# Keeping two weight blocks of a seven-product group in their buffers for a second use

## The chip, the cores and the metric

The kernel runs on one core of a Trainium2 chip. The metric is the device time of one execution in microseconds (us). The time before is the median of three runs, 2410.04 us (2409.96 to 2410.2).

## The reference

The reference is a decoder trunk of two layers in float32 with 512 positions and a model width of 1024. Each layer is a half-step SwiGLU feed-forward block, a parallel mixing of three attentions, and a second half-step feed-forward block. The change touches only the feed-forward blocks, of which there are four:

```python
def _swiglu(t, w_gate, w_up, w_down):
    return (jax.nn.silu(t @ w_gate) * (t @ w_up)) @ w_down

for l in range(DEPTH):                                   # DEPTH = 2
    f = _swiglu(_rmsnorm(h, ffn1_pre_g[l]), ffn1_w_gate[l], ffn1_w_up[l], ffn1_w_down[l])
    h = h + 0.5 * _rmsnorm(f, ffn1_post_g[l])
    ...                                                  # token mixing
    f = _swiglu(_rmsnorm(h, ffn2_pre_g[l]), ffn2_w_gate[l], ffn2_w_up[l], ffn2_w_down[l])
    h = h + 0.5 * _rmsnorm(f, ffn2_post_g[l])
```

The hidden width is 2816, that is 22 tiles of 128.

## The kernel before

**Split products.** Every matrix product is made of three matmuls of the type fp32r: each factor is split into a high part h and a low rest l, and `mm3` sums h·h, h·l and l·h (L205, L206, L207). For a weight, ScalarE casts the high part, `wh` (L179), and VectorE subtracts it from the raw weight to get `wl` (L180). Names in the trace carry the block of the network: a0 and a1 are the first feed-forward blocks of the two layers, c0 and c1 the second ones. The trace leaves buffer numbers out, so `ga`, `ua`, `da` stand for gate, up and down weights of a0 and a1, and `gc`, `uc`, `dc` for those of c0 and c1.

**Seven products in place of eight.** The first 16 hidden tiles are worked in two chunks of eight. In each chunk the gate product, the up product and the down product are made as a group of seven half-size products (a Strassen-like scheme of Winograd's form) in place of eight: `feature_products` and `feature_product` for gate (G) and up (U), `products` and `product` for down (D). Four feature groups and two down groups make up the chunks of one feed-forward block; the last six hidden tiles are worked plainly. The weight matrix of a group has four blocks, B00, B10, B01 and B11. The weight factor of each product is

| product n | factor | block fetched by the product | subtraction on VectorE (L315) |
|---|---|---|---|
| 0 | B00 | B00 | none |
| 1 | B10 | B10 | none |
| 2 | t = B01 - B00 | B01 (into t) and B00 | t |
| 3 | t = B11 - t | B11 | t |
| 4 | B11 | B11 | none |
| 5 | t - B00 (t as product 3 left it, result in the raw buffer) | B00 | raw |
| 6 | t = B10 - t | B10 | t |

Feature groups take the products in the order 0, 2, 1, 3, 4, 5, 6 (`ORDER`), down groups in the order 0 to 6. A feature product has 48 matmuls of 128x128 by 128x256, a down product 24 of 128x512.

**Units, buffers and the queue.** A `BlockUnit` is half a block: 512 KB, fetched by one DMA that SP issues (`block`, L293). Each product has two of them. `fetch` gets a buffer and issues the transfer; `load` makes the subtraction if there is one, splits the result (`split_from`), and calls `loaded`, which gives the buffer back and lets further transfers start:

```python
def loaded(self):
    self.raw = None
    Q.took(self.place, -1)
    Q.fetch_ahead()
```

The class `Queue` holds all products in the order of a written-out list, `PLAN`: G of chunk 0, U of chunk 0, G of chunk 1, U of chunk 1, then the seven products of D of chunk 0 and of chunk 1, two at a time between plain gate and up products of the hidden tiles 18 and 20. Before a product starts, `load_ahead` loads the weights of the next products, four units ahead. `fetch_ahead` issues transfers in the order of the units, and stops at the first unit whose ring has no room. There are two rings: `raw`, of two buffers, and `o`, of four buffers in the feature groups and two in the down groups. In a feature group the units take the places raw, o, o in turn; in a down group the first unit takes raw and the second o. The split weights `wh` and `wl` have four buffers each. The tile t is kept in two further buffers of the tag `o` over a group.

The order in which each engine works through its instructions is set when the kernel is built, by a scheduler that estimates times, and is fixed on the chip: each engine runs its own stream in order. It puts a few matmuls of a following product ahead of the last product of the one before.

**Taking the results away.** In feature groups, ScalarE copies finished sums (L762) or applies the activation, and VectorE adds or multiplies the others into `hr` (L764, L766, L771). In down groups, VectorE forms the sums of the first factors, `as` (L798 to L804), and adds products to `f` (L838, L842).

Of the kernel before, what the change touches and what calls it, by code (L numbers as in the profile page):

```python
# [22 lines left out]
def kernel(  # L23
# [39 lines left out]
    _, S, D = x.shape  # L63
# [3 lines left out]
    ND = D // P  # L67
# [35 lines left out]
    def stile(shape, tag, name, dt=F32R):  # L103
        return sb.tile(shape, dt, tag=tag, bufs=BUFS[tag], name=name)
# [4 lines left out]
    def pbank(tag, name):  # L109
        return ps.tile([P, S], F32, tag=tag, bufs=4, name=name)  # L110
# [92 lines left out]
    def mm3(pt, lh, ll, rh, rl, start, stop, free=False):  # L203

        nc.tensor.matmul(pt, lh, rh, start=start, stop=False, skip_group_check=free)  # L205
        nc.tensor.matmul(pt, lh, rl, start=False, stop=False, skip_group_check=free)  # L206
        nc.tensor.matmul(pt, ll, rh, start=False, stop=stop, skip_group_check=free)  # L207
# [24 lines left out]
    class Unit:  # L232


        def __init__(self, src, k0, nk, c0, ncol, name, scale=None):
            self.tags, self.place = ("wh", "wl"), "raw"
            self.src, self.k0, self.nk, self.c0, self.ncol, self.name, self.scale = src, k0, nk, c0, ncol, name, scale
            self.h = self.raw = None

        def waits(self):  # L240

            return self.raw is None and self.h is None

        def fetch(self):
            if not self.waits():
                return
            Q.took(self.place, 1)
            self.raw = stile([P, self.nk, self.ncol], self.place, "raw_" + self.name, F32)
            nc.sync.dma_start(self.raw[:], self.src[self.k0 * P:(self.k0 + self.nk) * P, self.c0:self.c0 + self.ncol]
                              .rearrange("(k p) c -> p k c", p=P))  # L250

        def load(self):
            if self.h is not None:
                return
            self.fetch()
            self.split_from(self.raw[:])
            self.loaded()
# [5 lines that stand above are left out]
# [11 lines left out]
    class BlockUnit(Unit):  # L274
# [9 lines left out]
        def __init__(self, n, src, rows, k0, nk, ncol, keep, name, place="raw"):  # L284
            super().__init__(src, k0, nk, 0, ncol, name)
            self.n, self.rows, self.keep, self.fetched, self.place = n, rows, keep, False, place

        def waits(self):
            return not self.fetched
# [6 lines left out]
        def fetch(self):  # L296
            if self.fetched:
                return
            self.fetched = True
            if self.n == 2:  # L300
                tc.keep_in_program_order(self.block(self.keep.get(self.k0), (0, 1)))
            Q.took(self.place, 1)
            self.raw = stile([P, self.nk, self.ncol], self.place, "raw_" + self.name, F32)
            self.block(self.raw[:], self.BLOCKS[self.n])

        def load(self):
            if self.h is not None:
# [282 lines left out]
    def ffn(l, src, wg, wu, wd, dst, name, spare, parked, plan, aside=None):  # L590
# [123 lines left out]
        def beside(gen, steps, every):  # L714

            for i, us_ in enumerate(gen):
                if i % every == every - 1:
                    next(steps, None)
                yield us_
# [55 lines left out]
        def feature_products(ci, up):  # L775

            w, nm = (wu if up else wg)[l, :, ci * FC * P:(ci + 1) * FC * P], f"{'gu'[up]}{name}_{ci}"
            keep = Keep(lambda k0: stile([P, 2, S], "o", f"t{nm}_{k0}", F32)[:])
            places = itertools.cycle(("raw", "o", "o"))
            for n in ORDER:  # L780
                uns = [BlockUnit(n, w, ND // 2, k, 2, S, keep, f"{nm}_{n}_{k}", next(places)) for k in range(0, ND // 2, 2)]
                run = lambda n=n, uns=uns: feature_product(ci, up, n, uns)
                early = ci == 0 and not up and n in ORDER[:4]
                yield uns, (lambda run=run: beside(run(), itertools.islice(st["some"], 1), 2)) if early else run
# [4 lines left out]
        def first_factor(ci, n):  # L789

            a = lambda i, j: hr[2 * ci + j][:, :, HALVES[i]]
            nm = f"{name}_{ci}_{n}"
            h, l = (stile([P, FC // 2, S // 2], "v", f"a{x}{nm}")[:] for x in "hl")
            if n == 2:
                st["s", ci] = stile([P, FC // 2, S // 2], "v", f"as{nm}", F32)[:]
            s = st.get(("s", ci))
            if n == 2:
                nc.vector.tensor_tensor(s, a(1, 0), a(1, 1), ALU.add)  # L798
            elif n == 3:
                nc.vector.tensor_tensor(s, s, a(0, 0), ALU.subtract)  # L800
            elif n == 4:
                nc.vector.tensor_tensor(s, a(0, 1), s, ALU.subtract)
            elif n == 5:
                nc.vector.tensor_tensor(s, a(0, 0), a(1, 0), ALU.subtract)  # L804
            src = (a(0, 0), a(0, 1), s, s, s, s, a(1, 1))[n]
            split(h, l, src)
            st["a", ci, n] = h, l

        def product(ci, n, uns):
            if n == 0 and ci == 0:  # L810
                RINGS["o"] = 2
                dst.begin()
            if n < 6:
                first_factor(ci, n + 1)
            if n in (0, 1, 2):
                st["b", SUM[n]] = [pbank("z", f"pd{name}_{ci}_{n}_{e}") for e in range(2)]
            pts = st["b", SUM[n]]
            if n == 1 and ci:
                for e in range(2):
                    nc.scalar.copy(pts[e][:], dst.fs[e][:, HF[0]])  # L820
            h, l = st["a", ci, n]
            opens, ends = n in (0, 2) or (n == 1 and not ci), n in (1, 4, 6)
            for un in uns:
                for k in range(un.nk):
                    kk = un.k0 + k
                    for e in range(2):
                        c = slice(e * P, (e + 1) * P)
                        mm3(pts[e][:], h[:, kk, c], l[:, kk, c], un.h[:, k], un.l[:, k], opens and kk == 0,
                            ends and kk == FC // 2 - 1, free=True)
                        yield 3 * S * PE_US  # L830
            if n == 0:
                return
            i, hf = TO[n]
            for e in range(2):
                f = dst.fs[2 * i + e][:, HF[hf]]
                if n == 1:
                    nc.scalar.copy(f, st["b", 0][e][:])
                    nc.vector.tensor_tensor(f, f, pts[e][:], ALU.add)  # L838
                elif ci == 0 and n in (2, 3, 6):
                    nc.scalar.copy(f, pts[e][:])  # L840
                else:
                    nc.vector.tensor_tensor(f, f, pts[e][:], ALU.add)  # L842

        def products(ci):

            keep = Keep(lambda k0: stile([P, 2, S], "o", f"bt{name}_{ci}_{k0}", F32)[:])
            w = wd[l, ci * FC * P:(ci + 1) * FC * P]
            for n in range(7):
                uns = [BlockUnit(n, w, FC // 2, k, 2, S, keep, f"d{name}_{ci}_{n}_{k}", ("raw", "o")[k // 2])
                       for k in range(0, FC // 2, 2)]  # L850
                yield uns, (lambda n=n, uns=uns: product(ci, n, uns))

        marks, made = {}, {}
# [16 lines left out]
        def queue(what):  # L870
            kind, n = what[0], what[1]
            if kind in "gu":
                if n not in made:
                    made[n] = plain(n)
                ms = (what[2],) if what[-1] in (0, 1) and len(what) == 3 else range(2)
                uns = made[n][kind == "u"]
                run = (lambda: gates(n, uns, ms)) if kind == "g" else (lambda: ups(n, uns, ms))
                Q.add(uns if ms[0] == 0 else [], run)
            elif kind == "a":
                Q.add([], lambda: iter(first_factor(n, 0) or ()))  # L880
            elif kind == "m":
                if name == "a0":
                    Q.add([], mem_stats)
            else:
                if what not in made:
                    made[what] = products(n) if kind == "d" else feature_products(n, kind == "U")
                for one in made[what]:
                    Q.add(*one)
                    break
# [746 lines left out]
```

## Time and profile before

| | before |
|---|---|
| median of 3 runs | 2410.04 us |
| the profiled execution | 2413.01 us, span 2411.3 us, granted clock 0.998 |
| TensorE busy | 2383.9 us (99%) |
| weight loads of TensorE busy | 2129.1 us (88%) |
| VectorE busy | 1865.6 us (77%) |
| ScalarE busy | 1357.8 us (56%) |
| DMA | 372.10 MB, 154 GB/s on average |
| transfers of the feed-forward weights | 512 KB each, 4.2 to 4.8 us from issue to landing (median) |

The profile is of one execution, which took longer than the median by 3 us. Busy time of TensorE is modelled, since matmuls overlap, so an idle time of TensorE is read from what it waited for. In the lists of instructions a time in brackets is the idle time of the engine just ahead of the instruction, and behind the arrow stands what ended it. The chain is followed from the last instruction back to what released each step.

### The profile page before, as it was taken

The numbers are of one execution on the slowest core, as the hardware profiler recorded it, in microseconds if no ns is written. First come the engines' busy times: TensorE is split into PE (matmuls) and PEld (weight loads), VectorE is DVE, ScalarE is ACT, GpSimd is POOL, SyncE is SP. The second block draws the span as 40 slices with busy tenths as digits, with TensorE's granted clock in tenths as the row PEclk, the third lists the DMA queues.
The fourth block names the chain that finished last, engine by engine and source line by source line (L and its number), as shares of the span: only waits on it lengthen the run. The fifth ranks groups of instructions, "written<-read, shape, count | busy, mean of one in ns | idle before, by whom it ended". The sixth has DMA issues, their size and how long they took to land.

```text
span 2411.3 us, 36506 instructions
## 1 busy us (share of the span) xinstructions
PE 2383.9 (99%) x14407; PEld 2129.1 (88%) x14407; DVE 1865.6 (77%) x2462; ACT 1357.8 (56%) x2137; POOL 81.5 (3%) x134
## 2 busy tenths in 40 slices
PE   9999999999999999999999999999999999999998
PEld 8998889888888899988899988889888888999887
DVE  8878877678776688788698788766778766887885
ACT  6555565567655555455554554656676655545554
POOL 1000000000110000000000000000001100000000
PEclk9999999999999999999999999999999999999999
DMA  6765454222223466655557655542222234676544
GB/s 236 229 198 185 157 193 140 79 71 71 82 68 114 149 217 201 209 174 176 186 183 227 202 184 174 189 118 71 71 88 74 63 127 150 200 230 198 176 156 157
DMA packets 249344, 372.10 MB, mean 154 GB/s; under 512 B 11450, under 2 KB 126162, under 8 KB 249172
## 3 DMA queue, kind: packets, MB, share of 16 engines
q1 hardware_dynamic: 249076, 369.74, 47.9%
q8 instruction: 113, 1.85, 0.3%
q14 instruction: 59, 0.48, 0.1%
q0 software_dynamic: 96, 0.03, 0.0%
HBM read 357.14 MB, written 12.58 MB: 153 GB/s over the span
## 4 chain that ended last, share of the span: by engine, by line
PE 84%; DVE 7%; DMA 4%; ACT 3%; issue 2%; SPq 0%; DVEq 0%; ACTq 0%
PE pg L205 3%; PE pg L206 3%; PE pg L207 3%; PE pda L206 3%; PE pda L207 3%; PE pda L205 3%; PE pdc L206 2%; PE pdc L207 2%; PE pdc L205 2%; PE pb L207 1%; PE pb L206 1%; PE pb L205 1%; DMA raw_wo<-in_w_out_dram 1%; PE pwc1g L205 1%; PE pwc0g L205 1%
## 5 line engine op out<-in xcount | busy, mean ns | idle before, releaser
L205 PE MATMUL pg<-us_a,wh_wg 128*128 128x512 f32 x384 | 151.7, 395 | 0.0
L206 PE MATMUL pg<-us_a,wh_wg 128*128 128x512 f32 x384 | 150.6, 392 | 0.0
L207 PE MATMUL pg<-us_a,wl_wg 128*128 128x512 f32 x384 | 150.5, 392 | 0.0
L206 PE MATMUL pda<-wl_da,aha 128*128 128x512 f32 x224 | 87.5, 391 | 0.7 <-DVE wl_da L180 0.7
L206 PE MATMUL pdc<-wl_dc,ahc 128*128 128x512 f32 x224 | 87.5, 391 | 0.5 <-DVE wl_dc L180 0.5
L207 PE MATMUL pdc<-wh_dc,alc 128*128 128x512 f32 x224 | 87.2, 389 | 0.0
L207 PE MATMUL pda<-wh_da,ala 128*128 128x512 f32 x224 | 87.2, 389 | 0.0
L180 DVE TENSOR_TENSOR wl_dc<-raw_dc,wh_dc 128x1024 fp32r<-128x1024 f32 x50 | 61.1, 1222 | 33.2 <-ACT wh_dc L179 32.6
L205 PE MATMUL pda<-wh_da,aha 128*128 128x512 f32 x224 | 86.5, 389 | 0.0
L205 PE MATMUL pdc<-wh_dc,ahc 128*128 128x512 f32 x224 | 86.5, 389 | 0.0
L207 PEld LDWEIGHTS pg<-us_a,wl_wg 128*128 128x128 f32 x384 | 72.7, 189 | 15.5
L205 PEld LDWEIGHTS pg<-us_a,wh_wg 128*128 128x128 f32 x384 | 73.0, 190 | 14.6
L206 PEld LDWEIGHTS pg<-us_a,wh_wg 128*128 128x128 f32 x384 | 72.9, 190 | 14.6
L179 ACT CAST wh_dc<-raw_dc 128x1024 fp32r<-128x1024 f32 x50 | 52.7, 1053 | 57.6 <-PE pdc L207 17.7
L183 DVE SCALAR_TENSOR_TENSOR wl_wg<-raw_wg,wh_wg 128x1024 fp32r<-128x1024 f32 x48 | 58.5, 1223 | 33.9 <-ACT wh_wg L182 33.6
L180 DVE TENSOR_TENSOR wl_da<-raw_da,wh_da 128x1024 fp32r<-128x1024 f32 x50 | 61.1, 1222 | 24.4 <-ACT wh_da L179 23.9
L179 ACT CAST wh_da<-raw_da 128x1024 fp32r<-128x1024 f32 x50 | 52.6, 1053 | 44.4 <-PE pda L207 17.6
L179 ACT CAST wh_uc<-raw_uc 128x1024 fp32r<-128x1024 f32 x44 | 46.2, 1049 | 51.0 <-PE pwc0u L206 12.6
L180 DVE TENSOR_TENSOR wl_uc<-raw_uc,wh_uc 128x1024 fp32r<-128x1024 f32 x44 | 53.8, 1222 | 25.6 <-ACT wh_uc L179 24.9
L179 ACT CAST wh_ua<-raw_ua 128x1024 fp32r<-128x1024 f32 x44 | 46.0, 1049 | 41.6 <-PE pwa1u L206 12.6
L180 DVE TENSOR_TENSOR wl_ua<-raw_ua,wh_ua 128x1024 fp32r<-128x1024 f32 x44 | 53.6, 1221 | 20.0 <-ACT wh_ua L179 19.3
L182 ACT ACTIVATE wh_wg<-raw_wg 128x1024 fp32r<-128x1024 f32 x48 | 50.8, 1061 | 26.6 <-PE pv L1044 13.5
(640 smaller groups left out, 8933.2 us busy)
## 6 DMA issues: line engine op xcount, KB each, us to landing
raw_da<-in_ffn_w_down_dram SPq DMA_DIRECT2D x74, 512.0 KB, 4.7
raw_dc<-in_ffn_w_down_dram SPq DMA_DIRECT2D x74, 512.0 KB, 4.8
raw_ga<-in_ffn_w_gate_dram SPq DMA_DIRECT2D x68, 512.0 KB, 4.5
raw_ua<-in_ffn_w_up_dram SPq DMA_DIRECT2D x68, 512.0 KB, 4.3
raw_gc<-in_ffn_w_gate_dram SPq DMA_DIRECT2D x68, 512.0 KB, 4.2
raw_uc<-in_ffn_w_up_dram SPq DMA_DIRECT2D x68, 512.0 KB, 4.3
raw_wg<-in_w_gate_dram SPq DMA_DIRECT2D x48, 512.0 KB, 3.5
raw_wo<-in_w_out_dram SPq DMA_DIRECT2D x24, 512.0 KB, 3.7
```

What stands on the lines that cost most here:

```text
L179: both = [nc.scalar.copy(h_ap, src)]
L180: make = lambda: nc.vector.tensor_tensor(l_ap, src, h_ap.bitcast(F32), ALU.subtract)
L182: both = [nc.scalar.activation(h_ap, src, AF.Copy, scale=scale)]
L183: make = lambda: nc.vector.scalar_tensor_tensor(l_ap, src, scale, h_ap.bitcast(F32), ALU.mult, ALU.subtract)
L205: nc.tensor.matmul(pt, lh, rh, start=start, stop=False, skip_group_check=free)
L206: nc.tensor.matmul(pt, lh, rl, start=False, stop=False, skip_group_check=free)
L207: nc.tensor.matmul(pt, ll, rh, start=False, stop=stop, skip_group_check=free)
```

## The change

In a feature group, product 2 uses the two raw buffers that product 0 filled with B00, and product 4 the two that product 3 filled with B11. In a down group, product 4 uses those of product 3; product 2 still fetches B00 again. A unit that gives its buffer on has an heir: when it is loaded it hands over the buffer in place of returning it, and the heir has no transfer of its own for it. The tile t is fetched as before. The turn of places raw, o, o now goes over the ten units that are left.

```diff
         def __init__(self, n, src, rows, k0, nk, ncol, keep, name, place="raw"):
             super().__init__(src, k0, nk, 0, ncol, name)
             self.n, self.rows, self.keep, self.fetched, self.place = n, rows, keep, False, place
+            self.heir = None
+
+        def inherits(self, un):
+            un.heir, self.place = self, None
...
             if self.n == 2:
                 tc.keep_in_program_order(self.block(self.keep.get(self.k0), (0, 1)))
+            if self.place is None:
+                return
             Q.took(self.place, 1)
             self.raw = stile([P, self.nk, self.ncol], self.place, "raw_" + self.name, F32)
             self.block(self.raw[:], self.BLOCKS[self.n])
+
+        def loaded(self):
+            if self.heir is None:
+                super().loaded()
+            else:
+                self.heir.raw, self.heir.place, self.raw = self.raw, self.place, None
...
-            places = itertools.cycle(("raw", "o", "o"))
+            places, had = itertools.cycle(("raw", "o", "o")), {}
             for n in ORDER:
-                uns = [BlockUnit(n, w, ND // 2, k, 2, S, keep, f"{nm}_{n}_{k}", next(places)) for k in range(0, ND // 2, 2)]
+                uns = [BlockUnit(n, w, ND // 2, k, 2, S, keep, f"{nm}_{n}_{k}", n in (2, 4) or next(places))
+                       for k in range(0, ND // 2, 2)]
+                if n in (2, 4):
+                    for un, of in zip(uns, had[n - 2 + (n == 4)]):
+                        un.inherits(of)
+                had[n] = uns
...
             for n in range(7):
                 uns = [BlockUnit(n, w, FC // 2, k, 2, S, keep, f"d{name}_{ci}_{n}_{k}", ("raw", "o")[k // 2])
                        for k in range(0, FC // 2, 2)]
+                if n == 4:
+                    for un, of in zip(uns, had):
+                        un.inherits(of)
+                had = uns
```

## The prediction

> **What bounds the kernel now.** I read the busy times first, then the chain that ended last, then the waits of TensorE, then windows of 40 us over the stages that hold the seven-product groups, and last the instructions of VectorE one by one around each wait. From the page, the busy times, the chain's shares and the DMA queue:
>
> ```profile
> PE 2383.9 (99%) x14407; PEld 2129.1 (88%) x14407; DVE 1865.6 (77%) x2462; ACT 1357.8 (56%) x2137; POOL 81.5 (3%) x134
> q1 hardware_dynamic: 249076, 369.74, 47.9%
> PE 84%; DVE 7%; DMA 4%; ACT 3%; issue 2%; SPq 0%; DVEq 0%; ACTq 0%
> ```
>
> TensorE is idle for 2411.3 - 2383.9 = 27.4 us in all, and the DMA engines are busy for less than half of the span. A change that takes transfers away and no matmul can gain only from these 27.4 us, and only from the part that stands in the touched stages. The waits of TensorE that stand there are these (the line with pdc holds one wait of 0.5 in c0's first down group and one of 0.8 in the rest of down, which has no groups):
>
> ```profile
> PE pdc L206 <- DVE wl_dc L180: 1.3, 2, 0.8
> PE pwa1g L207 <- DVE wl_ga L180: 1.2, 1, 1.2
> PE pda L206 <- DVE wl_da L180: 0.7, 1, 0.7
> PE pwc0g L207 <- DVE wl_gc L180: 0.7, 1, 0.7
> PE pwa0g L207 <- DVE wl_ga L180: 0.4, 1, 0.4
> PE pwc0u L205 <- DVE hrc L764: 0.2, 1, 0.2
> ```
>
> Each of them ends on VectorE, none on a DMA. The windows (busy time of PE, PEld, DVE, ACT, POOL, each with its count, then clock, DMA share, GB/s) give the same from the side of the idle time:
>
> ```profile
> 80.00:120.00 40.00, 39.43 (x326) 39.03 (x325) 31.92 (x38) 25.01 (x31) 0.00 (x0) 1.00 0.73 222
> 200.00:240.00 40.00, 39.31 (x184) 32.66 (x183) 34.59 (x33) 21.90 (x25) 0.00 (x0) 1.00 0.69 236
> 920.00:960.00 40.00, 40.00 (x335) 40.00 (x335) 30.72 (x30) 20.80 (x24) 0.00 (x0) 1.00 0.75 242
> 960.00:1000.00 40.00, 39.12 (x324) 38.72 (x323) 31.16 (x30) 18.73 (x22) 0.00 (x0) 1.00 0.66 200
> 2200.00:2240.00 40.00, 40.00 (x335) 39.97 (x334) 31.25 (x30) 22.29 (x27) 0.00 (x0) 1.00 0.56 184
> 1040.00:1080.00 40.00, 39.48 (x229) 34.65 (x228) 35.67 (x35) 18.46 (x21) 0.00 (x0) 1.00 0.56 198
> 1280.00:1320.00 40.00, 38.60 (x320) 38.20 (x319) 30.54 (x30) 17.78 (x21) 0.00 (x0) 1.00 0.67 204
> 2160.00:2200.00 40.00, 39.66 (x329) 39.26 (x328) 31.23 (x31) 18.44 (x22) 0.00 (x0) 1.00 0.68 203
> ```
>
> The idle time, 40 less PE's busy time, is 0.57 + 0.69 + 0.88 + 0.52 + 1.40 + 0.34 = 4.40 us. That is the most that the change can gain, and 0.18% of the run. The two windows without idle time hold 335 matmuls each, at a DMA share of 0.75 and of 0.56: the matmuls' own pace does not feel the transfers. So fewer bytes are worth nothing by themselves. What counts is when a weight's second factor (wl) is ready on VectorE.
>
> **What goes away.** A feature group loses four transfers of 512 KB (its third and its sixth product in order take over buffers), a down group two. Each of the four feed-forward blocks has four feature groups and two down groups, so 4 x (4 x 4 + 2 x 2) = 80 transfers, 42 MB of the 369.74 MB on the queue. No matmul, cast or subtraction goes or comes. By the rows above this costs and gains nothing directly. What it moves is the moment at which a buffer comes free, the moment of the next issue on SP, and the place that the scheduler then gives the subtractions (L315) in VectorE's in-order stream. I read these places off the built program's instruction order and price them on VectorE's timeline.
>
> **Where up meets gate (U of chunk 0, then G of chunk 1).** In c0 the timeline has, VectorE first, then one row of ScalarE, then two of the chain:
>
> ```profile
> 947.57 1.22 DVE L180 TENSOR_TENSOR wl_uc<-raw_uc,wh_uc 128x1024 fp32r<-128x1024 f32 x1
> ...
> 949.90 1.21 DVE L180 TENSOR_TENSOR wl_uc<-raw_uc,wh_uc 128x1024 fp32r<-128x1024 f32 x1
> 952.65 1.23 DVE L180 TENSOR_TENSOR wl_uc<-raw_uc,wh_uc 128x1024 fp32r<-128x1024 f32 x1 [1.53 <-ACT wh_uc L179]
> ...
> 958.68 1.23 DVE L315 TENSOR_TENSOR tgc<-tgc,raw_gc 128x1024 f32<-128x1024 f32 x1 [1.92 <-DMA raw_gc<-in_ffn_w_gate_dram]
> ...
> 961.56 1.22 DVE L315 TENSOR_TENSOR tgc<-tgc,raw_gc 128x1024 f32<-128x1024 f32 x1
> ...
> 965.68 1.22 DVE L180 TENSOR_TENSOR wl_gc<-raw_gc,wh_gc 128x1024 fp32r<-128x1024 f32 x1
> 966.82 1.28 DVE L764 TENSOR_TENSOR hrc<-hrc,pwc0u 128x512 f32<-128x512 f32 x2
> ```
> ```profile
> 963.09 1.05 ACT L179 CAST wh_gc<-raw_gc 128x1024 fp32r<-128x1024 f32 x1 [1.83 <-PE pwc0u L206]
> ```
> ```profile
> 956.79 4.25 DMA tgc<-in_ffn_w_gate_dram
> 967.55 0.39 PE pwc0u L205
> ```
>
> The cast of the next group's first weight is done at 963.09 + 1.05 = 964.14, yet its wl is made only from 965.68, because the two subtractions t = t - B00 at 958.68 and 961.56 (one waited 1.92 us for a DMA, and the queue behind it waited too) pushed the stream back. TensorE needs that wl for one matmul that the scheduler had put ahead of the last up product: the 0.7 us wait, and 0.2 us for the sum at 966.82 behind it.
>
> In the changed program both subtractions stand earlier: the first right behind the wl at 949.90, the second behind the one at 952.65. B00 needs no second transfer, and t's two transfers are released by the wl at 947.57 and at 949.90. With the 4.25 us of the tgc row, t lands at 947.57 + 1.22 + 4.25 = 953.0 and at 949.90 + 1.21 + 4.25 = 955.4. This adds a wait: VectorE, free at 951.1, stands until 953.0, and behind it is queued the wl now at 952.65, which moves to 954.2 and ends at 955.4. Who waits for that is the sixth product. Product seven begins at 967.55; less 0.9 us of waits, three matmuls ahead and 48 matmuls of 0.12 us (5.76), the sixth begins at about 960.5, so 5 us are spare. The wl after it ends at about 957.8, and its half begins at 963.4. By 958.4 VectorE has caught up. Two times 1.14 us then lie ahead of the congestion, the wl at 965.68 can start when its cast is done (964.2) and ends at 965.4, before TensorE comes to it (966.2). Besides, the matmul that needs it now stands behind the last product, 49 matmuls later. The 0.7 us go, in two independent ways. What is late next is the sum at 966.82, which can start no earlier than the matmuls that it reads are done; I take half of the 0.2 us as gone.
>
> The same reordering stands in all four blocks. Removed: 0.4 (a0) + 0.7 (c0) + 1.2 (a1) + 0 (c1, whose gate waits for no wl) = 2.3 us, and half of 4 x 0.2 = 0.4 us (the 0.2 is what the windows leave beside the wl waits of 0.4 and 1.2, and 0.34 in c1). Sum 2.7 us; bounds 1.5 and 3.2 (0.57 + 0.88 + 1.40 + 0.34).
>
> **Down, chunk 0.** Here VectorE is nearly full. Timeline, chain, and a window inside the burst of transfers:
>
> ```profile
> 1070.53 1.22 DVE L180 TENSOR_TENSOR wl_dc<-btc,wh_dc 128x1024 fp32r<-128x1024 f32 x1
> 1071.67 1.22 DVE L802 TENSOR_TENSOR asc<-hrc,asc 128x1024 f32<-128x1024 f32 x1
> 1072.80 1.22 DVE L315 TENSOR_TENSOR btc<-raw_dc,btc 128x1024 f32<-128x1024 f32 x1
> 1074.39 1.22 DVE L315 TENSOR_TENSOR raw_dc<-btc,raw_dc 128x1024 f32<-128x1024 f32 x1 [0.37 <-DMA raw_dc<-in_ffn_w_down_dram]
> 1075.54 1.22 DVE L180 TENSOR_TENSOR wl_dc<-btc,wh_dc 128x1024 fp32r<-128x1024 f32 x1
> ```
> ```profile
> 1064.62 0.37 SPq L293
> 1065.66 8.64 DMA raw_dc<-in_ffn_w_down_dram
> 1076.81 0.50 PE pdc L206
> ```
> ```profile
> 1066.00:1074.00 8.00, 8.00 (x37) 6.63 (x36) 7.80 (x8) 2.74 (x4) 0.00 (x0) 1.00 1.03 385
> ```
>
> Before, the second half of product 5 (issued 1065.66, landed 1074.30) is subtracted at 1074.39, ahead of wl of product 3 (1075.54), and TensorE waits 0.5 us for that. After, product 4 needs no transfer, product 5's first half takes its place on SP (issue about 1064.7), and its subtraction stands right behind the wl at 1070.53, ahead of the other subtraction (1072.80), of asc (1071.67) and of wl of product 3. VectorE is there at 1071.67. At 385 GB/s, 512 KB take 1.36 us; product 4's first half was two transfers ahead of the one landing at 1074.30, so it landed at 1074.30 - 2 x 1.36 = 1071.6. The added wait is about nothing, and three steps of 1.14 us later wl of product 3 starts at 1075.1, 0.4 us earlier than 1075.54. Its second half's wl comes about 0.8 us later than before, but two gate matmuls have been moved in front of it. I book 0.3 us gained over a0 and c0 together, of the 0.69 and 0.52 idle; bounds are +1.2 gained and the loss below. Down of chunk 1 has the same order and no wait of TensorE before; I take zero, with the same loss as a bound.
>
> **Sum.** 2.7 + 0.3 = 3.0 us off the profiled run of 2413.0 us, giving 2410.0. The profiled run is 3.0 us above the median of 2410.04, so the median goes to about 2407.0.
>
> **Rivals.** (1) Slower: product 5's first half lands late, with VectorE's stream standing behind its subtraction. If it takes the 8.64 us of the slowest row from 1065.0, it lands at 1073.6, 1.9 us after VectorE is there; less the 0.4 us of advance, wl of product 3 is 1.5 us later. With four blocks and two down groups each, the price is up to 8 x 1.5 = 12 us; with the 2.7 gained elsewhere that is 2410.0 + 9.3 = 2419.3 at worst, and 2416.3 with half of it in chunk 1's groups (4 x 1.5 + 4 x 0.75 - 2.7 = +6.3). It decides from a landing about 1 us late on average (8 x 1 - 2.7 = 5.3). For it: VectorE at 7.80 of 8 us, a0's and c0's existing waits. Against it: the place on the queue is product 4's, two ahead of the transfer that took 8.64 us. The Trainium skill (DMA: Bandwidth & Descriptors, Queues, rings and completion order) says that completion on one issuing queue need not be first in, first out; by that rule the earlier place promises nothing, and the landing could be as late as the burst's last. The rows shown here hold no two landings out of order, so this trace neither bears the rule out nor refutes it. (2) Nothing happens: the transfers were hidden, and the freed time on VectorE goes into other waits at the same places, 2410.0, or 2408.5 with the lower bound of 1.5. For it: the sum at 966.82 is right behind the wl. (3) Everything in the touched stages goes: 2410.0 - 4.4 = 2405.6. Against it: the sums must still be evacuated. (4) The buffers aren't taken over in all groups: then fewer than 80 transfers go; the built program has 80 fewer, so I give this no chance.
>
> **Chances.** Forecast (gain of 1.5 to 4.0) 0.53; nothing (within 1.5 either way) 0.20; everything 0.07; slower by (1) 0.20, of which 0.15 lie over the bound. A difference of 0.2%, 4.8 us, is about what a measurement of this kernel can tell from no change. Over that bound on the fast side I give 0.05, for idle time that the waits do not name; same 0.80. The range, 2405.0 to 2414.0, takes in (2), (3) and the milder half of (1).
>
> **What would show it.** Right: 80 transfers fewer; no wait of pwa0g, pwc0g, pwa1g for a wl; PE's idle time in 960 to 1000 below 0.3; a wait of tgc or tga for DMA of some 2 us on VectorE, earlier than before, that no PE wait follows. The down step is right if raw_d of product 5 is subtracted with less than 0.5 us of idle time before it. Wrong: a new PE wait on wl_d of product 3 or on wl_u of product 6 in order, a wait of over 1 us on raw_d ahead of L315, or another matmul count in windows without waits.

## The result, and the profile after

The change makes the kernel 0.2% faster: 2404.36 us (median of 20 runs, 2401.27 to 2407.39) against 2409.93 (20 runs, 2405.27 to 2412.84), a ratio of 0.9978 with a 95% interval of 0.9972 to 0.9984, so 3.9 to 6.7 us. A repetition gave 0.9980 (0.9971 to 0.9990). The direction was forecast; the size (3.0 us) and the low end of the range (2405.0) were not enough.

From the page of the full change, the counterparts of the busy times and the queue:

```profile
PE 2379.3 (99%) x14407; PEld 2127.5 (89%) x14407; DVE 1868.7 (78%) x2462; ACT 1356.5 (56%) x2137; POOL 81.5 (3%) x134
q1 hardware_dynamic: 227316, 327.79, 42.4%
```

The queue moved 369.74 - 327.79 = 41.95 MB less, which is 80 transfers of 512 KB. TensorE's busy time fell by 4.6 us although it has the same 14407 matmuls: a first sign that its busy time holds something that is not work. The windows of 40 us at the four places where up of chunk 0 meets gate of chunk 1:

```profile
80.00:120.00 40.00, 40.00 (x335) 39.97 (x335) 32.95 (x40) 24.51 (x31) 0.00 (x0) 1.00 0.54 164
960.00:1000.00 40.00, 40.00 (x335) 39.97 (x334) 31.73 (x30) 19.64 (x23) 0.00 (x0) 1.00 0.53 156
1280.00:1320.00 40.00, 40.00 (x335) 39.97 (x334) 33.03 (x32) 17.42 (x21) 0.00 (x0) 1.00 0.54 159
2160.00:2200.00 40.00, 40.00 (x335) 39.97 (x334) 30.08 (x28) 20.27 (x25) 0.00 (x0) 1.00 0.55 159
```

All four are without idle time and hold 335 matmuls, where before held 326, 324, 320 and 329. The start times of the same TensorE instructions in both profiles say the same: the full change gains 1.0, 1.3, 1.8 and 0.8 us at the four places, 4.9 us together. VectorE there, in c0 (this profile is 2.5 us ahead of that of before up to this place and 3.8 us ahead behind it, as the start times of the same ScalarE instructions in both show):

```profile
950.71 1.23 DVE L327 TENSOR_TENSOR tgc<-tgc,raw_gc 128x1024 f32<-128x1024 f32 x1 [2.20 <-DMA tgc<-in_ffn_w_gate_dram]
951.85 1.22 DVE L180 TENSOR_TENSOR wl_uc<-raw_uc,wh_uc 128x1024 fp32r<-128x1024 f32 x1
953.05 1.23 DVE L327 TENSOR_TENSOR tgc<-tgc,raw_gc 128x1024 f32<-128x1024 f32 x1
...
961.68 1.23 DVE L180 TENSOR_TENSOR wl_gc<-raw_gc,wh_gc 128x1024 fp32r<-128x1024 f32 x1 [0.76 <-ACT wh_gc L179]
962.88 1.41 DVE L776 TENSOR_TENSOR hrc<-hrc,pwc0u 128x512 f32<-128x512 f32 x2
```

Both subtractions of t stand early, VectorE waits 2.20 us for the first, nobody on TensorE waits for what is queued behind, and the wl of gate now waits for ScalarE's cast in place of VectorE's own queue. That is the mechanism as forecast. In down the waits stayed (waits of TensorE, full change):

```profile
PE pdc L206 <- DVE wl_dc L180: 0.7, 1, 0.7
PE pda L206 <- DVE wl_da L180: 0.5, 1, 0.5
```

### The profile page after: what moved, and what is told of

Its sections match the earlier page's. It is cut to its first block, busy times and chain, and to the rows that moved or that the text cites. A ratio compares the mean times of both kernels' runs of the same rounds, so it can differ in the third digit from the quotient of the medians.

```text
span 2402.7 us, 36336 instructions
## 1 busy us (share of the span) xinstructions
PE 2379.3 (99%) x14407; PEld 2127.5 (89%) x14407; DVE 1868.7 (78%) x2462; ACT 1356.5 (56%) x2137; POOL 81.5 (3%) x134
## 3 DMA queue, kind: packets, MB, share of 16 engines
q1 hardware_dynamic: 227316, 327.79, 42.4%
## 4 chain that ended last, share of the span: by engine, by line
PE 87%; DVE 6%; ACT 3%; DMA 3%; issue 1%; SPq 0%; DVEq 0%; ACTq 0%
PE pg L205 3%; PE pg L206 3%; PE pg L207 3%; PE pda L206 3%; PE pda L207 3%; PE pda L205 3%; PE pdc L206 2%; PE pdc L207 2%; PE pdc L205 2%; PE pb L207 1%; PE pb L206 1%; PE pb L205 1%; PE pwc0u L205 1%; PE pwc1u L205 1%; PE pwa1u L205 1%
```

## The experiments

**First: which groups bring it?** Four kernels take buffers over in some groups only. The edits go into the two lines with `n in (2, 4)` and the line `if n == 4` of down.

feats_only leaves out the three lines of down; down_only has `n in (2, 4) and False`; g1_only leaves out down and has

```diff
-                if n in (2, 4):
+                if n in (2, 4) and (ci == 1 and not up):
```

and all_but_g1 has `not (ci == 1 and not up)` and keeps down.

feats_only: 

> Only the feature groups take buffers over (64 transfers fewer), the down groups are as before. Theory A (the time comes from one place in each feed-forward block, where the last up product of chunk 0 meets the first gate product of chunk 1): -4.9 us, since the four windows around that place hold 326, 324, 320 and 329 matmuls before in place of 335, that is 41 matmuls of 0.119 us. Theory B (the time comes from the bytes, 5.6 us for 80 transfers, 0.07 us each): -4.5 us. Theory C (the down groups give or take): -5.6 less their share, so a gain clearly under 4 or over 6.

down_only: 

> Only the down groups take buffers over (16 transfers fewer). Theory A: 0 within 0.5 us, with TensorE still waiting 0.5 to 0.7 us for wl of product 3 in chunk 0 of a0 and c0. Theory B: -1.1 us. Theory C: whatever feats_only lacks to -5.6.

g1_only: 

> Only the gate group of chunk 1 takes buffers over, in each of the four blocks: 16 transfers fewer. Theory A: the whole -4.9 us, with 335 matmuls in each 40 us around the four places. Theory B: 16 x 0.07 = -1.1 us.

all_but_g1: 

> All groups take buffers over, but for the gate group of chunk 1: 64 transfers fewer. Theory A: 0 within 0.5 us, the waits for wl of gate (0.4, 0.7, 1.2) are still there. Theory B: 64 x 0.07 = -4.5 us.

Measured against before: feats_only 0.9985 (0.9976 to 0.9994), -3.6 us, with an interval (1.4 to 5.8 us faster) too wide to tell the three theories apart. down_only 1.0005 (0.9996 to 1.0014), not told from zero. g1_only 1.0016 (1.0007 to 1.0025), 3.9 us slower, with 16 transfers fewer. all_but_g1 1.0028 (1.0016 to 1.0040), 6.8 us slower, with 64 transfers fewer. Theory B (bytes) falls with the last two. Theory A in its simple form falls too: the gate group of chunk 1 alone puts VectorE's two subtractions early, but makes it worse. The timeline of VectorE in g1_only says why; it waits for both tiles t, and in the full change for the first alone:

```profile
952.16 1.23 DVE L327 TENSOR_TENSOR tgc<-tgc,raw_gc 128x1024 f32<-128x1024 f32 x1 [2.63 <-DMA tgc<-in_ffn_w_gate_dram]
...
958.35 1.23 DVE L327 TENSOR_TENSOR tgc<-tgc,raw_gc 128x1024 f32<-128x1024 f32 x1 [2.70 <-DMA tgc<-in_ffn_w_gate_dram]
```

and in its waits of TensorE the sums queued behind come late:

```profile
PE pwa0u L205 <- DVE hra L776: 2.0, 1, 2.0
PE pwc0u L205 <- DVE hrc L776: 1.7, 1, 1.7
PE pwc1u L205 <- DVE hrc L776: 1.5, 1, 1.5
PE pwa1u L205 <- DVE hra L776: 1.4, 1, 1.4
```

SP's issues of the second tile t in g1_only, and of both tiles in the full change (whose profile is 0.6 us ahead of that of g1_only there), say when the transfers could start:

```profile
954.55 0.37 SPq L297 DMA_DIRECT2D tgc<-in_ffn_w_gate_dram  x1
```
```profile
945.65 3.25 SPq L297 DMA_DIRECT2D tgc<-in_ffn_w_gate_dram  x2
```

With up of chunk 0 as before, buffers come free later, t lands after VectorE reaches its subtraction, and the added wait that was harmless in the full change stops TensorE. all_but_g1 keeps the waits for wl of gate (0.9, 0.5, 1.0) and adds four others of 1.0 to 1.5 us at the meetings of other groups.

**Second: which take-over, and which groups together?** Down stays as before in all three; `before_again` is the kernel before for a second profile.

```diff
-                if n in (2, 4):
+                if n in (2, 4) and up != ci:      # u0g1_only; n2_only has n == 2, n4_only has n == 4
```

u0g1_only: 

> The up group of chunk 0 and the gate group of chunk 1 take buffers over, 32 transfers fewer; where they meet, VectorE's order is that of the full change. Theory A2 (at that place both groups are needed: the gate group to put its two subtractions early, the up group so that SP can issue their transfers early; a stop of TensorE costs its wait plus about 0.27 us): -4.9 us there, with 335 matmuls in each of the four windows, and new waits only elsewhere. Theory B (0.07 us for each transfer): -2.2 us everywhere. Theory D (the gate group alone decides, and the loss of g1_only came from somewhere else): a loss as in g1_only, +4.6 us.

n2_only: 

> In all feature groups product 2 takes over, product 4 fetches again; down as before; 32 transfers fewer. VectorE's order where up of chunk 0 meets gate of chunk 1 is that of the full change. Theory A2: there the transfers of t are not issued earlier than the up group's own transfers allow, so waits of over 1 us for hr (L776) come back as in g1_only, about +2 us in all four against before at most, and no -4.9. Theory B: -2.2 us.

n4_only: 

> In all feature groups product 4 takes over, product 2 fetches again; down as before; 32 transfers fewer. TensorE's order is that of before, matmul for matmul. Theory A2: the matmul that needs wl of gate still stands ahead of the last up product and one subtraction still stands in the stretch ahead of that wl, so waits of 0.4 to 1.2 us for wl of gate stay, and the time is that of before within 1.5 us. Theory B: -2.2 us.

before_again: 

> The kernel before, unchanged, for a second profile of it: which steps of the comparison of two profiles stand in stages that no transfer was taken from. Theory A2: the steps at the start, near 590, near 1180 and near 1790 us (up to 1.8 us each) come and go from one execution to the next, and the four places where up meets gate stay within 0.5 us of the first profile.

u0g1_only is 1.0021 (1.0010 to 1.0031), n2_only 1.0035 (1.0021 to 1.0048), n4_only 1.0033 (1.0020 to 1.0045). In sum all three lose, but not in the same place. u0g1_only and n2_only have 332 or more matmuls in each of the four windows: where up meets gate they are as good as the full change. So theory A2 was right that the up group's take-over is needed beside the gate group's, and wrong on n2_only: product 2's take-over is enough for it. Their loss is a new stop at the end of gate of chunk 0 in all four blocks (waits of TensorE in n2_only; u0g1_only has the same four rows):

```profile
PE pwa0g L205 <- ACT sa L774: 1.9, 1, 1.9
PE pwc1g L205 <- ACT sc L774: 1.5, 1, 1.5
PE pwc0g L205 <- ACT sc L774: 1.5, 1, 1.5
PE pwa1g L205 <- ACT sa L774: 1.5, 1, 1.5
```

There the built kernel has matmuls of the sixth and fifth gate product interleaved in another order than before. n4_only keeps TensorE's order and has the waits for wl of gate, larger than before (1.6, 1.5, 0.9, 0.8). Theory A2 had put its time within 1.5 us of before; it is 8.0 us slower, and that forecast missed.

The second profile of before missed what I expected of it in part. The step at the start (1.4 us between the two profiles of before) and one near 1188 us (1.1 us, with a wait of 0.8 us for wl in the first) do come and go. Those near 590 and 1790 us stand in both; what they are is said at the end. But the loss that I meant to explain comes and goes as well: its four windows hold 331, 334, 316 and 335 matmuls.

```profile
960.00:1000.00 40.00, 39.97 (x334) 39.77 (x333) 30.56 (x30) 18.55 (x22) 0.00 (x0) 1.00 0.65 198
1280.00:1320.00 40.00, 38.15 (x316) 37.75 (x315) 31.70 (x32) 15.78 (x18) 0.00 (x0) 1.00 0.64 196
```

In the first profile of before 41 of 4 x 335 matmuls are missing there, in the second 24, in down_only (which leaves these groups alone) 33; at 40 / 335 = 0.119 us each that is 4.9, 2.9 and 3.9 us.

**Third: does the corrected theory predict a kernel?** n2_only was given product 4's take-over in gate of chunk 0 only, where its new stop was; g0u0g1 leaves out up of chunk 1 and down.

```diff
-                if n in (2, 4):
+                if n == 2 or n == 4 and (ci, up) == (0, False):   # n2_g0n4
...
-                if n in (2, 4):
+                if n in (2, 4) and (ci, up) != (1, True):         # g0u0g1
```

n2_g0n4: 

> n2_only with one thing more: in the gate group of chunk 0 product 4 takes over as well. TensorE's order is then that of before but for the one matmul moved in each block. 40 transfers fewer than before. Theory A3: the four waits of 1.5 to 1.9 us for ScalarE's sa and sc at the end of gate of chunk 0, which n2_only has, are gone (4 x 1.9 = 7.6 us with the 0.27 us of each stop), and the 335 matmuls where up meets gate stay: 3 to 5 us faster than before. Theory E (the half-changes are slower for their transfers, not for that order): as n2_only, about 8 us slower than before.

g0u0g1: 

> Both take-overs in the feature groups of gate 0, up 0 and gate 1, not in up 1, down as before; 48 transfers fewer. TensorE's order is before's but for the one matmul moved in each block. Theory A3: 3 to 5 us faster than before, unless the meeting of gate 1 and up 1 stops TensorE as it did in all_but_g1 (2 to 4 us for each block that does).

after_again: 

> The full change again, with a second profile. Theory A3 (product 2's take-over in the up group of chunk 0 and the gate group of chunk 1 takes the stop away where they meet; product 4's take-over keeps the other junctions as they were): faster than before by 3.5 to 6.5 us; 335 matmuls in each of the four windows again.

All three kernels came out as theory A3 said: n2_g0n4 0.9982 (0.9973 to 0.9991), g0u0g1 0.9981 (0.9971 to 0.9991), and the full change 0.9980 (0.9971 to 0.9990). Eight transfers fewer than in n2_only, two in each block, turn 8.4 us of loss into 4.3 us of gain, which bytes can't do. Theory A3 doesn't cover everything: n4_only and all_but_g1 stop at other junctions although product 4 takes over in most of their groups or in all, and why they do stays open. The windows of n2_g0n4:

```profile
80.00:120.00 40.00, 39.75 (x331) 39.55 (x330) 32.22 (x39) 24.33 (x30) 0.00 (x0) 1.00 0.63 187
960.00:1000.00 40.00, 40.00 (x335) 39.98 (x335) 31.66 (x30) 19.76 (x23) 0.00 (x0) 1.00 0.60 182
1280.00:1320.00 40.00, 40.00 (x335) 39.97 (x334) 33.16 (x33) 17.43 (x21) 0.00 (x0) 1.00 0.61 184
2160.00:2200.00 40.00, 40.00 (x335) 39.97 (x334) 29.98 (x28) 20.30 (x25) 0.00 (x0) 1.00 0.62 185
```

The whole of it in one table. Missing matmuls are those of 4 x 335 in the four windows; us are worked out from the ratio. The last column goes over the feature groups alone.

| kernel | transfers fewer | against before, us | missing matmuls (us at 0.119) | waits in other places of the feature groups that before has not |
|---|---|---|---|---|
| before, first and second profile | 0 | | 41, 24 (4.9, 2.9) | |
| full change | 80 | -5.3, again -4.8 | 0, 1 (0.1) | none |
| feats_only | 64 | -3.6 | 1 (0.1) | none |
| n2_g0n4 | 40 | -4.3 | 4 (0.5) | none |
| g0u0g1 | 48 | -4.6 | 6 (0.7) | none over 0.4 |
| down_only | 16 | +1.2 (-1.0 to +3.4) | 33 (3.9) | none |
| g1_only | 16 | +3.9 | 62 (7.4) | none over 0.5 |
| u0g1_only | 32 | +5.1 | 3 (0.4) | 1.9, 1.5, 1.5, 1.5, 0.7 for sa, sc |
| n2_only | 32 | +8.4 | 0 | the first four of these; 1.1 for wh |
| n4_only | 32 | +8.0 | 73 (8.7) | 1.1, 0.8, 0.7 for sa, sc |
| all_but_g1 | 64 | +6.8 | 40 (4.8) | 1.5 for wh; 1.4, 1.4, 1.0 for sa, sc |

Of the 73 missing matmuls of n4_only some 14 are none of its waits: in its window of c0, which holds 305, the granted clock is 0.50 for 3.4 us (968.2 to 971.6). Half of 3.4 us at 0.119 us each makes the 14, an estimate.

**Fourth: the stop in down.** pool3 is the full change with one sum moved:

```diff
             elif n == 3:
-                nc.vector.tensor_tensor(s, s, a(0, 0), ALU.subtract)
+                (nc.vector if ci else nc.gpsimd).tensor_tensor(s, s, a(0, 0), ALU.subtract)
```

pool3: 

> The full change with one more: in down of chunk 0 the sum as for product 3 is made by GpSimd in place of VectorE, four instructions of 1.1 us off VectorE's stream. If TensorE's waits there (0.5 and 0.7 us in a0 and c0, with 0.17 us of restart each) come from VectorE's full stream, they go, 1 to 1.5 us off the full change; if GpSimd takes over 4 us for the sum, the low part of the factor comes late and TensorE waits for that, 2 us or more slower.

It took back the gain: 1.0003 (0.9994 to 1.0011) against before, 5 to 6 us slower than the full change. GpSimd's group of instructions and TensorE's waits:

```profile
L817 POOL TENSOR_TENSOR asc<-asc,hrc 128x1024 f32<-128x1024 f32 x2 | 6.8, 3382 | 651.9 <-ACT wh_gc L179 651.9
```
```profile
PE pdc L206 <- DVE wl_dc L180: 3.3, 3, 1.7
PE pda L206 <- DVE wl_da L180: 2.6, 2, 1.3
```

The sum takes 3.4 us there in place of 1.2, still under the 4 us that I had set as the limit, and the waits grew from 1.2 to 5.9 us. The low part of the factor now stands later in VectorE's stream (at 1069.75 in c0) and the wl that TensorE waits for comes behind it, at 1074.30. So taking 1.1 us off VectorE here is not worth 1.1 us; that its stream is too full in this stage was not refuted by this.

## Why the prediction was wrong in size, point by point

**The step that failed is "The idle time, 40 less PE's busy time, is ... That is the most that the change can gain".** It took the idle time of TensorE in a window as the loss, and so the term of the four places where up meets gate, booked at 2.7 us with a bound of 3.2, came out at 4.9. The list of TensorE's instructions in before, across the stop in c0, shows the error:

```profile
965.89 0.28 PE L205 MATMUL pwc0g<-us_b,wh_gc 128*128 128x256 f32 x1
966.01 0.28 PE L206 MATMUL pwc0g<-us_b,wh_gc 128*128 128x256 f32 x1
966.96 0.38 PE L207 MATMUL pwc0g<-us_b,wl_gc 128*128 128x256 f32 x1 [0.66 <-DVE wl_gc L180]
967.55 0.39 PE L205 MATMUL pwc0u<-us_b,wh_uc 128*128 128x256 f32 x1 [0.22 <-DVE hrc L764]
967.78 0.28 PE L206 MATMUL pwc0u<-us_b,wh_uc 128*128 128x256 f32 x1
967.90 0.28 PE L207 MATMUL pwc0u<-us_b,wl_uc 128*128 128x256 f32 x1
```

Matmuls start 0.12 us apart and each row is 0.28 us long or more, since they overlap. Idle time is counted from the end of a row, so a stop shows less than it costs. From 966.01 to 967.78 there are three steps that take 1.77 us in place of 0.36: a loss of 1.41 us, of which the brackets show 0.88. The full change has no such gap: its window holds 335 matmuls. In c1 the prediction put the wait for wl at zero, since no row there shows one, and booked 0.1 us in all:

```profile
2163.96 0.28 PE L206 MATMUL pwc1g<-us_b,wh_gc 128*128 128x256 f32 x1
2164.36 0.39 PE L207 MATMUL pwc1g<-us_b,wl_gc 128*128 128x256 f32 x1
2164.96 0.39 PE L205 MATMUL pwc1u<-us_b,wh_uc 128*128 128x256 f32 x1 [0.21 <-DVE hrc L764]
2165.19 0.28 PE L206 MATMUL pwc1u<-us_b,wh_uc 128*128 128x256 f32 x1
```

The matmul with wl stands 0.40 us behind the one before it, without a bracket, and the three steps take 1.23 us in place of 0.36: a loss of 0.87 us, of which the brackets show 0.21. Counting matmuls gives the loss without this error, as long as the granted clock stays at 1.00, and the counts stood in the rows of the prediction: 335 - 326, 324, 320 and 329 are 9, 11, 15 and 6, 41 in all, 4.9 us in place of the 3.2 that I took as the upper bound of this term. So did the busy time of the weight loads: 40 less 39.03, 38.72, 38.20 and 39.26 is 4.8 us. The Trainium skill (Perfetto Trace Analysis, Identifying the Most-Contended Engine) says that matmul busy time is no good measure of how close a kernel is to the roofline, because pipelined instructions look smaller in the trace, and sends its reader to the busy share of weight loads, and to the share of the peak FLOP rate that a kernel reaches. Here the trace agrees, to 0.1 us in 4.9. Idle time falls short of the loss in the two other profiles with these groups as before too: 2.1 us of idle time against 2.9 us by count in the second profile of before, and 2.3 against 3.9 in down_only. That the loss went past the bound of 3.2 us, and not only past the booked 2.7, is a matter of the execution: in one of the three it did not.

**Where up meets gate: right in mechanism, too small in size.** Booked 2.7 us (0.5, 0.8, 1.3 and 0.1 in a0, c0, a1 and c1); the loss that is gone was 4.9 (1.0, 1.3, 1.8 and 0.8) in the profile I used, and 2.9 to 4.9 over three profiles that have these groups as before. The sum at 966.82, of whose 0.2 us I took half, cost nothing any more in any of the four blocks. That the gain has "two independent ways" was not shown: no kernel here moved the matmul and left the subtractions, or the reverse. The added wait of VectorE was forecast to end at 953.0 and, with the 2.5 us added back, ended at 953.2; the 5 us spare covered it.

**Down: booked at 0.3 us, found at nothing that can be told.** Product 5's first half landed in time (its subtraction follows the wl without idle time), so rival (1) fell. But wl of product 3 started at 1071.66, which is 0.07 us earlier than before, not 0.4:

```profile
1059.87 1.23 DVE L327 TENSOR_TENSOR btc<-btc,raw_dc 128x1024 f32<-128x1024 f32 x1 [0.74 <-DMA raw_dc<-in_ffn_w_down_dram]
...
1068.25 1.22 DVE L327 TENSOR_TENSOR raw_dc<-btc,raw_dc 128x1024 f32<-128x1024 f32 x1
1069.39 1.22 DVE L327 TENSOR_TENSOR btc<-raw_dc,btc 128x1024 f32<-128x1024 f32 x1
1070.53 1.22 DVE L819 TENSOR_TENSOR asc<-hrc,asc 128x1024 f32<-128x1024 f32 x1
1071.66 1.22 DVE L180 TENSOR_TENSOR wl_dc<-btc,wh_dc 128x1024 fp32r<-128x1024 f32 x1
```

The step was right that one wait of 0.37 us for a DMA goes; the first subtraction of the group waited 0.32 us longer (0.74 in place of 0.42) and gave it back. Second profile of before: 0.3 us of wait in c0 and none listed in a0, so this term also varies by itself more than I booked.

**Rivals and cover.** Rival (3), everything in the touched stages, came true where gate and up meet, and its price of 4.4 us was short for the same reason as the sum. The statement that bytes are worth nothing by themselves stands: transfers fewer and time do not go together in the table.

**What stays open.** 5.3 us were measured for the full change, 3.9 to 6.7 by its interval; the meeting of up and gate explains 2.9 to 4.9, on average of the three profiles 3.9. In the repetition the mean granted clock of the full change was 0.9982 against 0.9979 for before, which by estimate (0.0003 of 2411 us) is 0.7 us of its 4.8; the rest, 4.1 us, lies within what the meeting explains. For the first 5.3 us the clocks of before aren't on record, and what lies over 4.9 is not told from nothing.

n2_only lost 8.4 us (5.1 to 11.6). By the start times of TensorE's instructions against the first profile of before, its four stops at the end of gate of chunk 0 cost 2.2, 1.8, 1.8 and 1.8 us, and what follows them 1.0 (with the wait of 1.1 for wh), 0.4, 0.4 and 0.4, 9.7 us in all; less 2.9 to 4.9 gained where up meets gate, that is 4.8 to 6.8. The mean granted clock of its five runs was 0.9966 against 0.9978 for before, by estimate (0.0012 of 2411 us) 2.9 us more. The two make 7.7 to 9.7, which takes in the 8.4; five runs are few for the second term, and the profile is of the fastest of the five (2415.31 against a median of 2420.18).

## What to carry to other kernels

Price a stop of a pipelined engine by the instructions that are missing in a window at full pace, or by the starts of the instructions, not by the idle time between rows, and look first whether the granted clock was full there. A saved transfer is worth what its buffers and its place in the in-order queues do to the next weights; a take-over in half of the groups can cost more than none. Before a wait of a few tenths of a microsecond is made the basis of a sum, take a second profile of the same kernel: it may not be there.

## What the runs showed of the hardware that was not expected

A subtraction of 128x1024 float32 takes 3.38 us on GpSimd and 1.22 us on VectorE. In a timeline of TensorE a stop can cost 0.28 us and show no idle time at all (the matmul with wl in c1 above).

In stages outside the change two profiles of one kernel differ by steps of up to 1.6 us. One, near 1188 us at the end of down in c0, is a wait of 0.8 us for wl in the one and none in the other. Others are stretches of 3.4 us in which the granted clock is 0.50. The first profile of before has them at 598 and 1796 us, its second at 8, 595 and 1790, the full change at 595 in its first profile and at 1203 in its second. The 3 us from 1796 in the first profile of before, then in that of the full change:

```profile
1796.00:1799.00 3.00, 3.00 (x9) 2.41 (x8) 2.30 (x6) 2.58 (x6) 0.00 (x0) 0.50 0.00 0
1796.00:1799.00 3.00, 3.00 (x17) 2.62 (x16) 1.62 (x3) 2.95 (x6) 0.20 (x1) 1.00 0.67 212
```

By the start times of the same TensorE instructions the full change gains 1.6 us there that are not its own. What sets the clock back is not shown.
